# A two-layer fp32 trunk with split weights: the low part of one weight tile in four made by an accumulating DMA

## The chip, the cores and the metric

One core of a Trainium2 chip runs the whole program as one launch. The metric is the device time of one execution in microseconds (us).

## The reference

`x` is a residual stream of 256 tokens by 2048 channels; there are two layers. In each, the RMS-normalised input is projected by one matrix of 20480 columns into the parts of two token mixers and two gates. Differential attention (8 heads of two softmaxes each) and stick-breaking attention (16 heads) run beside each other; each result is gated by SiLU and projected to 2048 channels; the two are merged by sigmoid gates and projected once more onto the residual:

```python
h = rms_norm(x, norm_gain)
(da_q, da_k, da_v, da_z, sb_q, sb_k, sb_v, sb_z, gate_a, gate_b) = split_columns(h @ w_in)   # 10 x 2048
oa = differential_attention(rope(rms_norm(q)), rope(rms_norm(k)), va, lam)
ua = (rms_norm(oa) * (1 - lambda_init)) * silu(da_z)
ub = stick_breaking_attention(qs, ks, vs) * silu(sb_z)
y = sigmoid(gate_a) * (ua @ w_branch_a) + sigmoid(gate_b) * (ub @ w_branch_b)
x = x + y @ w_out
```

All inputs, weights and outputs are float32.

## The kernel before

The program is written for a tile framework: it names tiles in pools with so many slots each, and a scheduler sets the order of instructions on each engine and the semaphores between them. A slot of a pool is used again when all readers of its old tile are done.

**Numbers in three products.** Each float32 operand of a matmul is held as a high part (the value cast to float32r) and a low part (value minus high part, again float32r). `mm3` (lines 64 to 67) sums three products in PSUM: high x high (L65), high x low (L66) and low x high (L67).

**Weights.** All weight matrices lie in HBM as tiles of 128 partitions by 1024 float32 (512 KB): two 128-row blocks of 512 output columns. `load_w` (lines 76 to 88) takes one such tile through three steps: SyncE loads it into `wraw` (L83), ScalarE casts it to the high part `wh` (L61), VectorE subtracts to get the low part `wl` (L62). `wraw` has four slots, `wh` and `wl` three each; the split stands at a higher priority than its place in the program.

**Projections.** `project` (lines 90 to 107) computes 256 tokens by 512 columns. It walks through 8 weight tiles (kp = 0 to 7), each used for 12 matmuls of 128x128 by 128x512: two 128-row blocks, two token tiles, three products. In the text "tile 0" to "tile 7" of a projection are these. There are 104 projections, 52 per layer, one after the other: for each of four column groups the q, k, v and z parts of differential attention; then for each group q, k, z and v of stick-breaking attention; then, for each of four column groups, gate a with `w_a`, then gate b with `w_b`; then four of `w_o`. The attention work of a group (scores, softmax, transposes) is put by the scheduler among the matmuls of the projections that follow. The stages are called differential attention, stick-breaking attention, merge and output below.

**GpSimd** has little to do: the small chains `rv`, `rr` of the norms (L127, L130), two of the products of the rotary embedding (`tok`, L260 and L262), and eight stores of the next layer's input (`x_next`, L480). `work` holds six slots of token tiles `tok` (128x512).

Of the kernel before, what the change touches and what calls it, by code (L numbers as in the profile page):

```python
# [9 lines left out]
F32 = mybir.dt.float32  # L10
F32R = mybir.dt.float32r
AF = mybir.ActivationFunctionType
ALU = mybir.AluOpType
# [3 lines left out]
P = 128  # L17
# [5 lines left out]
CW = 512  # L23
NG = D // CW
KK = 2
# [13 lines left out]
def trunk(ctx: ExitStack, tc: tile.TileContext, x, xT, gT, norm_gain, w_in, qk_gain, lam_vecs,  # L39
          subln, w_a, w_b, w_o, rope_cs, out):  # L40
    nc = tc.nc

    const = ctx.enter_context(tc.tile_pool(name="const", bufs=1))
    big = ctx.enter_context(tc.tile_pool(name="big", bufs=1))
    wp = ctx.enter_context(tc.tile_pool(name="wp", bufs=3))
    att = ctx.enter_context(tc.tile_pool(name="att", bufs=1))
    work = ctx.enter_context(tc.tile_pool(name="work", bufs=6))
    small = ctx.enter_context(tc.tile_pool(name="small", bufs=4))
    dram = ctx.enter_context(tc.tile_pool(name="dram", bufs=1, space=bass.MemoryType.DRAM))
    ps_mm = ctx.enter_context(tc.tile_pool(name="ps_mm", bufs=4, space=PSUM))  # L50
# [3 lines left out]
    def heads(ap):  # L54
        return ap.rearrange("p (h d) -> p h d", d=HD)
# [4 lines left out]
    def split(h, l, src):  # L60
        nc.scalar.copy(h, src)  # L61
        nc.vector.tensor_tensor(out=l, in0=src, in1=h.bitcast(F32), op=ALU.subtract)  # L62

    def mm3(ps, lh, ll, rh, rl, start, stop):
        nc.tensor.matmul(ps, lhsT=lh, rhs=rh, start=start, stop=False)  # L65
        nc.tensor.matmul(ps, lhsT=lh, rhs=rl, start=False, stop=False)  # L66
        nc.tensor.matmul(ps, lhsT=ll, rhs=rh, start=False, stop=stop)  # L67
# [5 lines left out]
    gcol = const.tile([P, KT], F32, name="gcol")  # L73
    nc.scalar.dma_start(out=gcol, in_=gT)

    def load_w(src, parts=1, between=None):
        raw = wp.tile([P, KK * CW], F32, name="wraw", bufs=4)
        h = wp.tile([P, KK * CW], F32R, name="wh")
        l = wp.tile([P, KK * CW], F32R, name="wl")
        n = KK * CW // parts  # L80
        for i in range(parts):
            c = slice(i * n, (i + 1) * n)
            nc.sync.dma_start(out=raw[:, c], in_=src[:, c])  # L83
            if between is not None and i == 0:
                between()
            with tc.high_priority(offset=400):
                split(h[:, c], l[:, c], raw[:, c])
        return h, l
# [20 lines left out]
    def pair(tag):  # L109
        return (big.tile([P, KT, S], F32R, name=tag + "h", tag=tag + "h"),  # L110
                big.tile([P, KT, S], F32R, name=tag + "l", tag=tag + "l"))

    def put_T(src, dst, c, t):
        """Four 128x128 blocks of src, transposed and split, into k-tiles 4c.. of dst."""
        tr = ps_tr.tile([P, CW], F32, name="tr")
        for j in range(CW // P):
            nc.tensor.transpose(out=tr[:, j * P:(j + 1) * P], in_=src[:, j * P:(j + 1) * P],  # L117
                                identity=ident)
        js, ts = slice(c * 4, c * 4 + 4), slice(t * P, (t + 1) * P)
        trv = heads(tr)  # L120
        split(dst[0][:, js, ts], dst[1][:, js, ts], trv)

    def rsqrt_mean(ss, n):
        """(ss / n + eps) ** -0.5"""
        w = ss.shape[1]
        v = small.tile([P, 4], F32, name="rv")
        nc.gpsimd.tensor_scalar(out=v[:, :w], in0=ss, scalar1=1.0 / n, scalar2=RMS_EPS,  # L127
                                op0=ALU.mult, op1=ALU.add)
        r = small.tile([P, 4], F32, name="rr")
        nc.gpsimd.tensor_tensor(out=r[:, :w], in0=v[:, :w], in1=mhalf[:, :w], op=ALU.pow)  # L130
        return r[:, :w]

# [1 line left out]
    xt = pair("xT")  # L134
    ss_part = small.tile([P, NT, NG], F32, name="ss_part", bufs=2)
    sq_junk = const.tile([P, CW], F32, name="sq_junk")
# [45 lines left out]
    for l in range(DEPTH):  # L182
        lam_init = 0.8 - 0.6 * math.exp(-0.3 * l)

# [1 line left out]
        rope = {}  # L186
        g4 = work.tile([P, CW], F32, name="tok")
        nc.sync.dma_start(out=g4, in_=qk_gain[l:l + 1, :].broadcast_to([P, CW]))
# [23 lines left out]
        nc.vector.tensor_tensor(out=nlam, in0=le[:, 1:2], in1=le[:, 0:1], op=ALU.subtract)  # L212
        nc.vector.tensor_scalar(out=nlam, in0=nlam, scalar1=-lam_init, scalar2=None, op0=ALU.add)

# [1 line left out]
        ssx = small.tile([P, NT], F32, name="ssx", bufs=2)  # L216
        nc.vector.tensor_reduce(out=ssx, in_=ss_part, axis=AX.X, op=ALU.add)
        rstd = small.tile([P, NT], F32, name="rstd", bufs=2)
        nc.vector.tensor_copy(rstd, rsqrt_mean(ssx, D))
        rstd_s = small.tile([P, NT], F32, name="rstd_s", bufs=2)  # L220
        nc.vector.tensor_scalar(out=rstd_s, in0=rstd, scalar1=QK_SCALE, scalar2=None, op0=ALU.mult)
# [73 lines left out]
            return gz  # L295

        def scores(qT, kT, hs, t, mask):
            """Masked scores of heads hs for query tile t: [128, len(hs) * keys]."""
            nk = (t + 1) * P
            sc = ps_sc.tile([P, CW], F32, name="sc")  # L300
            for i, h in enumerate(hs):
                ts = slice(t * P, (t + 1) * P)
                mm3(sc[:, i * nk:(i + 1) * nk], qT[0][:, h, ts], qT[1][:, h, ts],
                    kT[0][:, h, :nk], kT[1][:, h, :nk], True, True)
            w = len(hs) * nk
            sm = work.tile([P, CW], F32, name="tok")
            mk = mask[:, S - nk:].unsqueeze(1).broadcast_to([P, len(hs), nk])
            nc.vector.tensor_tensor(out=sm[:, :w].rearrange("p (h k) -> p h k", k=nk),
                                    in0=sc[:, :w].rearrange("p (h k) -> p h k", k=nk),
                                    in1=mk, op=ALU.add)  # L310
            return sm, nk

        def attn_pair():
            """Transposed weights, split: per head the blocks (query tile, key tile) 00, 10, 11."""
            return (att.tile([P, HPG, 3, P], F32R, name="aTh"),
                    att.tile([P, HPG, 3, P], F32R, name="aTl"))

        def attn_T(a, aT, hs, t):
            """a: [128, heads hs, key tiles 0..t] of query tile t."""
            tr = ps_tr.tile([P, CW], F32, name="tr")  # L320
            w = len(hs) * (t + 1) * P
            for j in range(0, w, P):
                nc.tensor.transpose(out=tr[:, j:j + P], in_=a[:, j:j + P], identity=ident)  # L323
            hh, bb = slice(hs[0], hs[-1] + 1), slice(t, 2 * t + 1)
            split(aT[0][:, hh, bb], aT[1][:, hh, bb],
                  tr[:, :w].rearrange("p (h b k) -> p h b k", b=t + 1, k=P))

# [1 line left out]
        for g in range(NG):  # L329
            qT = da_qk("q", g)  # L330
            kT = da_qk("k", g)
            aT = attn_pair()
            for t in range(NT):
                nk = (t + 1) * P
                for hs in ([[0, 1, 2, 3]] if t == 0 else [[0, 1], [2, 3]]):
                    sm, _ = scores(qT, kT, hs, t, masks["causal"])
                    n = len(hs)
# [5 lines left out]
                    sums = small.tile([P, HPG], F32, name="sums")  # L343
# [8 lines left out]
                    a = work.tile([P, CW], F32, name="tok")  # L352
# [31 lines left out]
                nc.vector.tensor_tensor(out=u, in0=hold[:, t], in1=gz[:, t], op=ALU.mult)  # L384
                put_T(u, ua, g, t)

# [1 line left out]
        for g in range(NG):  # L388
            qT = sb_qk("q", g)
            kT = sb_qk("k", g)  # L390
# [2 lines left out]
            for t in range(NT):  # L393
                for hs in ([[0, 1, 2, 3]] if t == 0 else [[0, 1], [2, 3]]):
                    sm, nk = scores(qT, kT, hs, t, masks["strict"])
                    e = work.tile([P, CW], F32, name="tok")
                    nc.scalar.activation(out=e, in_=sm, func=AF.Abs)
                    nc.scalar.activation(out=e, in_=e, func=AF.Exp, scale=-1.0)
                    nc.scalar.activation(out=e, in_=e, func=AF.Ln, bias=1.0)
                    rl = work.tile([P, CW], F32, name="tok")  # L400
                    nc.vector.tensor_scalar(out=rl, in0=sm, scalar1=0.0, scalar2=None, op0=ALU.max)
                    for i in range(len(hs)):
                        lo, hi = i * nk, (i + 1) * nk
                        rv = slice(hi - 1, lo - 1 if lo else None, -1)
                        nc.vector.tensor_tensor_scan(out=e[:, rv], data0=e[:, rv], data1=rl[:, rv],
                                                     initial=0.0, op0=ALU.add, op1=ALU.add)
                    nc.vector.tensor_tensor(out=sm, in0=sm, in1=e, op=ALU.subtract)
                    nc.scalar.activation(out=sm, in_=sm, func=AF.Exp)
                    attn_T(sm, wT, hs, t)
            gz = act_proj(SB_Z, g, AF.Silu)  # L410
            gzT = att.tile([P, HPG, S], F32, name="gzT", tag="hold")
            for t in range(NT):
                tr = ps_tr.tile([P, CW], F32, name="tr")
                for h in range(HPG):
                    nc.tensor.transpose(out=tr[:, h * P:(h + 1) * P],  # L415
                                        in_=gz[:, t, h * P:(h + 1) * P], identity=ident)
                nc.scalar.copy(gzT[:, :, t * P:(t + 1) * P], heads(tr))
            vh, vl = v_proj(SB_V, g)
            for hp in range(0, HPG, 2):
                o = ps_sc.tile([P, CW], F32, name="sc")  # L420
                ov = o.rearrange("p (h q) -> p h q", q=S)
                for i in range(2):
                    h = hp + i
# [9 lines left out]
                ks = slice(g * 4 + hp, g * 4 + hp + 2)  # L433
                split(ub[0][:, ks], ub[1][:, ks], uv)

# [1 line left out]
        ya = [att.tile([P, NT, CW], F32, name="ya", tag=tag) for tag in ("qTh", "qTl", "kTh", "kTl")]  # L437
        for c in range(NG):
            gz = act_proj(GATE_A, c, AF.Sigmoid)
# [11 lines left out]
                nc.vector.tensor_tensor(out=y, in0=y, in1=ya[c][:, t], op=ALU.add)  # L451
                put_T(y, yT, c, t)

# [1 line left out]
        last = l == DEPTH - 1  # L455
        if not last:
            x_next = dram.tile([S, D], F32, name="x_next")
# [2 lines left out]
        for c in range(NG):  # L460
# [7 lines left out]
            for t in range(NT):  # L468
                xn = work.tile([P, CW], F32, name="tok")
                n = 2 if last and c == NG - 1 and t == NT - 1 else 1  # L470
                for i in range(n):
# [3 lines left out]
                    if last:  # L475
                        eng = nc.scalar if i else nc.sync
                        eng.dma_start(out=out[t * P:(t + 1) * P, c * CW + w.start:c * CW + w.stop],
                                      in_=xn[:, w])
# [60 lines left out]
```

## Time and profile before

| | |
|---|---|
| time, median of 2 runs | 2438.73 us (2438.55 to 2438.91) |
| span of the profiled execution | 2436.2 us |
| TensorE busy | 2427.0 us (100%), 11328 matmuls |
| VectorE busy | 1430.3 us (59%) |
| ScalarE busy | 1257.7 us (52%) |
| GpSimd busy | 179.7 us (7%) |
| moved by DMA | 453.39 MB, mean 186 GB/s |

The profiled execution's own time is its span, 2436.2 us from the first to the last instruction; it lies 2.5 us under the median of the runs. In the rows of the profile PE is TensorE (PEld its weight loads), DVE is VectorE, ACT is ScalarE, POOL is GpSimd, SP is SyncE, and a q behind a name is the queue that issues DMAs. A row of a group gives line, engine, operation, output<-input, count, then busy time and mean ns of one, then the idle time before it and what ended that. A row of the timeline gives start, duration, engine, line, and in brackets the idle time before it with its releaser.

### The profile page before, as it was taken

The page shows a single profiled execution, that of the slowest core. Times are in us where ns is not written, and L with a number is a line of the kernel's source. Part 1 is how long each engine was busy: PE and PEld are TensorE (multiplying, and loading weights), DVE is VectorE, ACT ScalarE, POOL GpSimd, SP SyncE. Part 2 cuts the span into 40 slices and gives each one's busy share as a digit, 9 for nine tenths or more (in the row PEclk, how much of TensorE's full clock was granted, in tenths as well). Part 3 has the DMA queues.
Part 4 walks back from the last instruction along what each step waited for, and adds up shares of the span by engine and source line. Part 5 has one row for each costly group of instructions (what it writes and reads, how often), then busy time and mean ns, then how long its engine had stood idle before and what let it go on. Part 6 is the DMA issues. An engine that isn't in the chain of part 4 may idle for free.

```text
span 2436.2 us, 29977 instructions
## 1 busy us (share of the span) xinstructions
PE 2427.0 (100%) x11328; PEld 2019.4 (83%) x11328; DVE 1430.3 (59%) x1636; ACT 1257.7 (52%) x1771; POOL 179.7 (7%) x183
## 2 busy tenths in 40 slices
PE   9999999999999999999999999999999999999999
PEld 7888888888888888888888888888888888888887
DVE  7676766655656444555566757656556564445554
ACT  6555655645645444444455555556556454444443
POOL 2031130000000000000030321300000000000000
PEclk9999999999999999999999999999999999999999
DMA  8555555555555555556755555555555555555565
GB/s 291 170 174 179 173 179 179 175 176 171 172 179 174 196 191 195 191 192 201 240 199 173 176 179 173 173 182 173 173 174 173 182 173 192 196 191 191 189 206 182
DMA packets 128386, 453.39 MB, mean 186 GB/s; under 512 B 14321, under 2 KB 15089, under 8 KB 128241
## 3 DMA queue, kind: packets, MB, share of 16 engines
q1 hardware_dynamic: 127312, 449.24, 55.5%
q8 instruction: 89, 1.46, 0.3%
q0 software_dynamic: 640, 2.10, 0.2%
q14 instruction: 57, 0.46, 0.1%
q10 hardware_dynamic: 288, 0.14, 0.0%
HBM read 447.23 MB, written 4.19 MB: 185 GB/s over the span
## 4 chain that ended last, share of the span: by engine, by line
PE 99%; DMA 0%; SPq 0%; DVE 0%; ACT 0%; issue 0%; DVEq 0%
PE mm L66 31%; PE mm L67 31%; PE mm L65 31%; PE tr L117 2%; PE sc L67 1%; PE sc L66 1%; PE sc L65 1%; PE tr L323 1%; PE tr L415 0%; DMA wraw<-in_w_in 0%; DVE wl L62 0%; ACT wh L61 0%; SPq L148 0%; SPq L83 0%; SPq L141 0%; DVE tok L473 0%
## 5 line engine op out<-in xcount | busy, mean ns | idle before, releaser
L62 DVE TENSOR_TENSOR wl<-wraw,wh 128x1024 fp32r<-128x1024 f32 (+1 forms) x833 | 1026.3, 1232 | 838.1 <-ACT wh L61 837.5
L61 ACT CAST wh<-wraw 128x1024 fp32r<-128x1024 f32 (+1 forms) x833 | 875.7, 1051 | 969.8 <-PE mm L67 946.0
L66 PE MATMUL mm<-wl,xTh 128*128 128x512 f32 x2560 | 1004.6, 392 | 0.5 <-DVE wl L62 0.5
L67 PE MATMUL mm<-wh,xTl 128*128 128x512 f32 x2560 | 1004.6, 392 | 0.0
L65 PE MATMUL mm<-wh,xTh 128*128 128x512 f32 x2560 | 930.4, 392 | 4.6 <-DVE xTh L149 4.4
L65 PEld LDWEIGHTS mm<-wh,xTh 128*128 128x128 f32 x2560 | 480.5, 188 | 101.7 <-ACT wh L61 5.3
L66 PEld LDWEIGHTS mm<-wl,xTh 128*128 128x128 f32 x2560 | 481.5, 188 | 96.7 <-DVE wl L62 1.1
L67 PEld LDWEIGHTS mm<-wh,xTl 128*128 128x128 f32 x2560 | 481.5, 188 | 95.4
L66 PE MATMUL mm<-wl,uah 128*128 128x512 f32 x512 | 199.6, 390 | 0.0
L67 PE MATMUL mm<-wh,ual 128*128 128x512 f32 x512 | 199.3, 389 | 0.0
L65 PE MATMUL mm<-wh,uah 128*128 128x512 f32 x512 | 180.1, 390 | 0.0
L65 PEld LDWEIGHTS mm<-wh,uah 128*128 128x128 f32 x512 | 96.1, 188 | 19.9
L67 PEld LDWEIGHTS mm<-wh,ual 128*128 128x128 f32 x512 | 96.1, 188 | 19.8
L66 PEld LDWEIGHTS mm<-wl,uah 128*128 128x128 f32 x512 | 96.1, 188 | 19.7
L66 PE MATMUL mm<-wl,ubh 128*128 128x512 f32 x256 | 99.6, 389 | 0.0
L67 PE MATMUL mm<-wh,ubl 128*128 128x512 f32 x256 | 99.6, 389 | 0.0
L65 PE MATMUL mm<-wh,ubh 128*128 128x512 f32 x256 | 89.2, 389 | 0.0
L480 POOL DMA_DIRECT2D x_next<-tok x8 | 4.5, 567 | 828.8 <-DVE tok L473 828.8
L127 POOL TENSOR_SCALAR rv<-ssq 128x4 f32<-128x4 f32 (+1 forms) x48 | 26.7, 556 | 523.7 <-ACT sq_junk L372 272.5
L117 PEld LDWEIGHTS tr<-ident,tok 128*128 128x128 f32 x416 | 51.2, 140 | 12.5
L117 PE MATMUL tr<-ident,tok 128*128 128x128 f32 x416 | 60.9, 272 | 0.0
L130 POOL TENSOR_TENSOR rr<-rv,mhalf 128x4 f32<-128x4 f32 (+1 forms) x50 | 57.9, 1157 | 4.2
(115 smaller groups left out, 1524.8 us busy)
## 6 DMA issues: line engine op xcount, KB each, us to landing
wraw<-in_w_in SPq DMA_DIRECT2D x639, 512.0 KB, 3.3
wraw<-in_w_a SPq DMA_DIRECT2D x64, 512.0 KB, 3.3
wraw<-in_w_b SPq DMA_DIRECT2D x64, 512.0 KB, 3.3
wraw<-in_w_o SPq DMA_DIRECT2D x64, 512.0 KB, 3.9
tok<-in_x SPq DMA_DIRECT2D x8, 256.0 KB, 6.8
xr<-in_x SPq DMA_DIRECT2D x4, 512.0 KB, 5.6
x_next<-tok POOLq DMA_DIRECT2D x8, 256.0 KB, 5.2
xr<-x_next SPq DMA_DIRECT2D x4, 512.0 KB, 5.4
```

Source lines behind the costliest of these rows:

```text
L61: nc.scalar.copy(h, src)
L62: nc.vector.tensor_tensor(out=l, in0=src, in1=h.bitcast(F32), op=ALU.subtract)
L65: nc.tensor.matmul(ps, lhsT=lh, rhs=rh, start=start, stop=False)
L66: nc.tensor.matmul(ps, lhsT=lh, rhs=rl, start=False, stop=False)
L67: nc.tensor.matmul(ps, lhsT=ll, rhs=rh, start=False, stop=stop)
L117: nc.tensor.transpose(out=tr[:, j * P:(j + 1) * P], in_=src[:, j * P:(j + 1) * P], identity=ident)
L127: nc.gpsimd.tensor_scalar(out=v[:, :w], in0=ss, scalar1=1.0 / n, scalar2=RMS_EPS, op0=ALU.mult, op1=ALU.add)
L130: nc.gpsimd.tensor_tensor(out=r[:, :w], in0=v[:, :w], in1=mhalf[:, :w], op=ALU.pow)
L323: nc.tensor.transpose(out=tr[:, j:j + P], in_=a[:, j:j + P], identity=ident)
L480: nc.gpsimd.dma_start(out=x_next[t * P:(t + 1) * P, cs], in_=xn)
```

## The change

One weight tile in four gets its low part in another way. ScalarE casts the raw tile to `wh` as before, then writes minus `wh` into `wl`; then GpSimd issues a DMA that adds the raw values onto `wl`, so that `wl` holds raw minus high. For every second of these tiles the DMA reads the values from HBM again, for the others from the `wraw` slot in SBUF. The count starts so that these are tiles 0 (from HBM) and 4 (from SBUF) of each projection; the very first tile of the program, which is loaded in two pieces, is split as before. That makes 103 tiles of the first kind and 104 of the second. `wh` and `wl` have four slots, `wraw` three, and `work` five.

```diff
-    wp = ctx.enter_context(tc.tile_pool(name="wp", bufs=3))
+    wp = ctx.enter_context(tc.tile_pool(name="wp", bufs=4))
...
-    work = ctx.enter_context(tc.tile_pool(name="work", bufs=6))
+    work = ctx.enter_context(tc.tile_pool(name="work", bufs=5))
...
+    loads = [0]
+
     def load_w(src, parts=1, between=None):
-        raw = wp.tile([P, KK * CW], F32, name="wraw", bufs=4)
+        raw = wp.tile([P, KK * CW], F32, name="wraw", bufs=3)
         h = wp.tile([P, KK * CW], F32R, name="wh")
         l = wp.tile([P, KK * CW], F32R, name="wl")
         n = KK * CW // parts
+        loads[0] += 1
+        if parts == 1 and loads[0] % 4 == 1:
+            nc.sync.dma_start(out=raw, in_=src)
+            with tc.high_priority(offset=400):
+                nc.scalar.copy(h, raw)
+                nc.scalar.mul(l, h.bitcast(F32), -1.0)
+                if loads[0] % 8 == 1:
+                    nc.gpsimd.dma_start(out=l, in_=src, accum_op=ALU.add)
+                else:
+                    nc.gpsimd.dma_start(out=l, in_=raw, accum_op=ALU.add)
+            return h, l
         for i in range(parts):
```

What else the diff holds takes out comments. Line numbers of the changed kernel are 10 to 13 higher than those of before.

**ScalarE, in the merge stage** (`wh_` and `wl_` are numbered weight tiles, `gz` the gate's activation; a bracket names whose semaphores an instruction waits for, DMAHW those of loads, DMASW those of GpSimd's DMAs). Before, casts of weight tiles follow each other:

```order
L61 CAST wh_7121<-wraw_7120 128x1024 [waits DMAHW0_49,DVE_49,PE_49]
L61 CAST wh_7144<-wraw_7143 128x1024 [waits DMAHW1_49,DVE_49,PE_49]
L61 CAST wh_7162<-wraw_7161 128x1024 [waits DMAHW2_49,DVE_49,PE_49]
L294 ACTIVATE gz_7138<-mm_6992,rstd_357 128x512 [waits PE_49]
L61 CAST wh_7180<-wraw_7179 128x1024 [waits DMAHW3_49,DVE_49,PE_49]
```

Now, at the same place, the first cast of the projection (L87) has the negated copy (L88) behind it:

```order
L61 CAST wh_7190<-wraw_7189 128x1024 [waits DMAHW0_49,DVE_49,PE_49]
L87 CAST wh_7213<-wraw_7212 128x1024 [waits DMAHW1_49,PE_49,Activation_49]
L88 ACTIVATE wl_7214<-wh_7213 128x1024 [waits DMASW4_49,Activation_49]
L61 CAST wh_7232<-wraw_7231 128x1024 [waits DMAHW2_49,DVE_49,PE_49]
L61 CAST wh_7250<-wraw_7249 128x1024 [waits DMAHW3_49,DVE_49,PE_49]
L307 ACTIVATE gz_7207<-mm_7059,rstd_358 128x512 [waits PE_49]
```

The negated copy stands right behind its cast, and what followed the cast comes one instruction later.

**SyncE, the loads at the same place.** Before, each load of a raw tile waits for VectorE, the last reader of the slot's old tile:

```order
L83 DMA wraw_7102<-in_w_in 128x1024 [waits DMAHW3_49,DVE_49]
L83 DMA wraw_7120<-in_w_in 128x1024 [waits DMAHW4_49,DVE_49]
L83 DMA wraw_7143<-in_w_a 128x1024 [waits DMAHW5_49,DVE_49]
L83 DMA wraw_7161<-in_w_a 128x1024 [waits DMAHW6_49,DVE_49]
L83 DMA wraw_7179<-in_w_a 128x1024 [waits DMAHW7_49,DVE_49]
```

Now (L85 loads tiles 0 and 4, L96 the others; the row with `wraw_7134` is a tile 4, the row with `wraw_7212` the next tile 0):

```order
L85 DMA wraw_7134<-in_w_in 128x1024 [waits DMAHW2_49,DVE_49]
L96 DMA wraw_7153<-in_w_in 128x1024 [waits DMAHW3_49,DVE_49]
L96 DMA wraw_7171<-in_w_in 128x1024 [waits DMAHW4_49,DVE_49]
L96 DMA wraw_7189<-in_w_in 128x1024 [waits DMAHW6_49,DVE_49]
L85 DMA wraw_7212<-in_w_a 128x1024 [waits DMAHW5_49,DMASW4_49]
L96 DMA wraw_7231<-in_w_a 128x1024 [waits DMAHW7_49,DVE_49]
```

The load of the next tile 0 waits for a DMA of GpSimd, the one that read the raw tile 4, and the loads behind it wait with it. It is so for tile 0 in 70 of 103 projections; in the other 33 the load of tile 7 has that wait, and tile 0 stands behind it.

**GpSimd, in differential attention after a k projection.** Before (`rv` and `rr` are the norm of one token tile each, `tok` the rotary products):

```order
L127 TENSOR_SCALAR rv_1424<-ssq_1419 128x4 [waits Activation_49]
L130 TENSOR_TENSOR rr_1426<-rv_1424,mhalf_318 128x4 [waits Pool_49]
L260 TENSOR_TENSOR tok_1434<-tok_1430,t1_k_340 128x4x64 [waits DMAHW3_49,DVE_49]
L262 TENSOR_TENSOR tok_1434<-tok_1430,t1_k_340 128x4x64
L127 TENSOR_SCALAR rv_1450<-ssq_1445 128x4 [waits Activation_49]
L130 TENSOR_TENSOR rr_1452<-rv_1450,mhalf_318 128x4 [waits Pool_49]
L260 TENSOR_TENSOR tok_1460<-tok_1456,t1_k_340 128x4x64 [waits DVE_49,PE_49]
L262 TENSOR_TENSOR tok_1460<-tok_1456,t1_k_340 128x4x64
```

Now (L90 is the DMA of the next projection's tile 0, L92 that of its tile 4):

```order
L90 DMA wl_1576<-in_w_in 128x1024 [waits DMASW2_49,PE_49,Activation_49]
L140 TENSOR_SCALAR rv_1435<-ssq_1430 128x4 [waits Activation_49]
L143 TENSOR_TENSOR rr_1437<-rv_1435,mhalf_319 128x4 [waits Pool_49]
L140 TENSOR_SCALAR rv_1461<-ssq_1456 128x4 [waits Activation_49]
L143 TENSOR_TENSOR rr_1463<-rv_1461,mhalf_319 128x4 [waits Pool_49]
L273 TENSOR_TENSOR tok_1445<-tok_1441,t1_k_341 128x4x64 [waits DVE_49]
L275 TENSOR_TENSOR tok_1445<-tok_1441,t1_k_341 128x4x64
L92 DMA wl_1649<-wraw_1647 128x1024 [waits DMASW3_49,DMAHW3_49,PE_49,Activation_49]
L273 TENSOR_TENSOR tok_1471<-tok_1467,t1_k_341 128x4x64 [waits DVE_49,Pool_49]
L275 TENSOR_TENSOR tok_1471<-tok_1467,t1_k_341 128x4x64
```

The second token tile's `rv` and `rr` have moved ahead of the first one's products, and the DMA of tile 4 stands between the products of the first and of the second token tile.

## The prediction

> **What bounds the kernel now.** I read the page's busy table, the clock line and the chain of waits first.
>
> ```profile
> PE 2427.0 (100%) x11328; PEld 2019.4 (83%) x11328; DVE 1430.3 (59%) x1636; ACT 1257.7 (52%) x1771; POOL 179.7 (7%) x183
> ...
> PEclk9999999999999999999999999999999999999999
> ...
> PE 99%; DMA 0%; SPq 0%; DVE 0%; ACT 0%; issue 0%; DVEq 0%
> ```
>
> TensorE is busy 2427.0 of 2436.2 us at full granted clock, and 99% of the chain is TensorE. The change leaves every matmul in place. So the most it can win is the 9 us in which TensorE is not busy (0.4%), and what it can lose is open: a weight tile that comes late stops TensorE for as long as it is late. Everything below is therefore about lateness. The two groups that prepare a weight tile come next, with what they wait for, and then the rhythm in the merge stage, where nothing else mixes in.
>
> ```profile
> L62 DVE TENSOR_TENSOR wl<-wraw,wh 128x1024 fp32r<-128x1024 f32 (+1 forms) x833 | 1026.3, 1232 | 838.1 <-ACT wh L61 837.5
> L61 ACT CAST wh<-wraw 128x1024 fp32r<-128x1024 f32 (+1 forms) x833 | 875.7, 1051 | 969.8 <-PE mm L67 946.0
> ```
>
> ```profile
> 1102.93 0.61 PE L65 MATMUL mm<-wh,xTh 128*128 128x512 f32 x2
> 1103.13 1.05 ACT L61 CAST wh<-wraw 128x1024 fp32r<-128x1024 f32 x1 [1.67 <-PE mm L67]
> ...
> 1103.38 0.39 PE L66 MATMUL mm<-wl,xTh 128*128 128x512 f32 x1
> ...
> 1104.21 1.23 DVE L62 TENSOR_TENSOR wl<-wraw,wh 128x1024 fp32r<-128x1024 f32 x1 [1.50 <-ACT wh L61]
> ...
> 1105.65 0.61 PE L65 MATMUL mm<-wh,xTh 128*128 128x512 f32 x2
> ```
>
> Both preparing engines wait: ScalarE for TensorE to leave a slot (946 us), VectorE for ScalarE (837.5 us). Neither is near its limit. A tile lasts 1105.65 - 1102.93 = 2.72 us on TensorE. The cast of a new tile starts 0.20 us after TensorE has moved to the next one (a slot came free), and the low part is first needed 0.45 us into its tile (the L66 at 1103.38). With three slots the cast at 1103.13 serves the tile that starts two tiles after 1102.93, at 1108.37; its low part is done at 1105.44, so each tile is ready about 3.4 us before it is needed.
>
> **The change, part by part.** There are 832 tiles (833 splits, the first tile in two pieces), 8 to a projection, 104 projections. Tile 0 of each projection but the first takes its low part by an accumulating DMA from HBM (103 times), tile 4 of each by one from the raw tile in SBUF (104 times).
>
> *Removed from VectorE:* 207 subtractions of 1.23 us, 255 us. VectorE waits already; worth nothing.
>
> *Added to ScalarE:* 207 negated copies. The nearest row is the cast of the same shape, 1.05 us, so 217 us, which the 946 us of waiting for TensorE hides; if that cover were gone, all 217 us would show. What counts is that 1.05 us stands in each accumulated tile's chain.
>
> *Four slots instead of three:* the cast may start when TensorE has three tiles to go: budget 3 x 2.72 + 0.45 = 8.61 us from a tile's start to the need. From it go 0.20 (slot), 1.05 (cast), 1.05 (negated copy) and about 0.1 for two hand-overs (the row pair 1103.13 + 1.05 to 1104.21 shows 0.03 for one). **So the accumulating DMA has 6.2 us from its issue to land**, where the subtraction needed 1.23. That is the first number that decides.
>
> *How long it takes.* Before has no accumulating DMA. Its nearest rows, from the table of DMA issues, the issue line of L480, and the last 16 us (no load in flight any more):
>
> ```profile
> q1 hardware_dynamic: 127312, 449.24, 55.5%
> ...
> wraw<-in_w_in SPq DMA_DIRECT2D x639, 512.0 KB, 3.3
> ...
> x_next<-tok POOLq DMA_DIRECT2D x8, 256.0 KB, 5.2
> ...
> out<-tok SPq DMA_DIRECT2D x7, 256.0 KB, 5.9
> ```
>
> ```profile
> DMA to landing us min/median/max: 4.7/5.2/7.0
> ```
>
> ```profile
> out<-tok SPq DMA_DIRECT2D x1, 256.0 KB, 2.6
> ```
>
> Queue q1 moved 449.24 MB in 55.5% of 2436.2 us of the 16 engines, 332 GB/s, so 512 KB is 1.58 us and 256 KB 0.79 us of transfer. GpSimd's own plain store of 256 KB took 5.2 us beside weight loads. An accumulating 512 KB must read its source and its old destination; I count that as two transfers, 3.16 us, or 2.4 more than the store: 5.2 + 2.4 = **7.6 us** beside loads. The same store from SyncE fell from 5.9 to 2.6 us where no load ran, so alone I count 2.6 + 2.4 = 5.0 us. The ends I keep: 3.3 us (a plain load of that size, no extra cost) and 7.0 + 2.4 = 9.4 us (the slowest store). The form that reads the raw tile runs about half of its time beside loads, since with three raw slots SyncE then has no free slot: the middle of 5.0 and 7.6, **6.3 us**. The form that reads HBM runs beside the loads that were held back: 7.6 us.
>
> The Trainium skill puts a GpSimd-issued DMA at about 2.0 us plus bytes / 436 GB/s ("DMA: Bandwidth & Descriptors", "Anatomy of one DMA — SWDGE (gpsimd) path"), and says of the adding unit that it costs a second source read and no cycles of its own ("Collectives: The Full Stack", "The bandwidth ceiling: the fold count and why AG ≠ RS ≠ AR"). By both the accumulate would be an estimated 2.0 + 2.4 = 4.4 us and nearly all of the loss below would vanish. The x_next row disagrees with the first: 5.2 us where that formula gives 2.6.
>
> *Tile 4 (raw form):* 6.3 against 6.2: 0.1 us late, 104 x 0.1 = 10 us.
>
> *Three raw slots, and tile 4 holds its slot until its DMA has landed.* By the order on SyncE, 70 times the next tile 0 takes that slot, and 33 times tile 7 does, with tile 0 queued behind it. Tile 4 lands when TensorE needs it; call that 0. In the 70: load 3.4, cast 1.05, negated copy and hand-overs 1.2: the HBM-form DMA is issued at 5.7, and TensorE wants the result four tiles later, at 10.9: budget 5.2. At 7.6 it is 2.4 us late: 70 x 2.4 = 168 us. In the 33 the load is second in line behind tile 7's (1.58 more) and budget is 3.7: 33 x 3.9 = 129 us.
>
> *GpSimd's queue in differential attention.* After a q or k projection of that branch (16 of them) the order puts tile 4's DMA of the next projection behind two rv/rr pairs and two tok products. The rows of layer 1's first q, whose projection ended at 1242.7:
>
> ```profile
> 1242.71 0.37 ACT L241 ACTIVATE sq_junk<-mm,rstd 128x128 f32<-128x128 f32 x1 [0.53 <-PE mm L67]
> ...
> 1247.75 0.37 ACT L241 ACTIVATE sq_junk<-mm,rstd 128x128 f32<-128x128 f32 x1
> 1248.02 0.20 ACT L241 ACTIVATION_READ_ACCUMULATOR sq_junk<-mm,rstd 128x1 f32 x1
> ```
>
> ```profile
> 1245.53 0.87 POOL L127 TENSOR_SCALAR rv<-ssq 128x4 f32<-128x4 f32 x1 [19.99 <-ACT sq_junk L241]
> 1246.48 1.01 POOL L130 TENSOR_TENSOR rr<-rv,mhalf 128x4 f32<-128x4 f32 x1
> 1248.68 1.59 POOL L260 TENSOR_TENSOR tok<-tok,t_q 128x256 f32<-128x256 f32 x1 [1.19 <-issue]
> 1250.24 1.19 POOL L262 TENSOR_TENSOR tok<-tok,t_q 128x256 f32<-128x256 f32 x1
> 1251.51 0.69 POOL L127 TENSOR_SCALAR rv<-ssq 128x4 f32<-128x4 f32 x1
> 1252.29 1.86 POOL L130 TENSOR_TENSOR rr<-rv,mhalf 128x4 f32<-128x4 f32 x1
> ```
>
> The second rv can start when the second squares end, 1248.2; with 0.69, 1.86, 1.59 and 1.19 behind it the DMA is issued at about 1253.6, 10.9 us after the projection's end; the need is 4 x 2.72 + 0.45 = 11.3 after it. 10.9 + 6.3 - 11.3 = 5.9 us late, 5.8 more than counted: 16 x 5.8 = 93 us. Behind the waiting DMA stand the other two tok products, whose k or q TensorE needs later.
>
> *Against it: attention work.* Between tiles TensorE also has 2427.0 - 832 x 2.72 = 164 us of scores, transposes and values in the 64 attention projections, 2.56 us each. It lengthens budgets; about half falls into tile 0's chain (4 tiles of 8): -82 us.
>
> *Five work tiles for six:* each reuse of a token tile may wait sooner; on VectorE and ScalarE with over 800 us of slack I count nothing; a late transpose would cost up to the 82 us above.
>
> Sum: 10 + 168 + 129 + 93 - 82 = 318 us. The profiled span is 2436.2; the median of the two runs, 2438.7, lies 2.5 above it. 2438.7 + 318 = **2757 us**, 13% slower.
>
> **Rivals.** *In time (not slower).* The DMA without the contention that I put in lands in 5.0 us or less, in both forms. For it: the 2.6 us store when alone, and the 3.3 us load; against it: the 5.2 us of the only GpSimd DMAs here. Tile 4 is then 1.2 us early, which frees the raw slot earlier; budgets become 6.4 and 4.9, and tile 0 is in time. What is left is GpSimd's queue, 16 x (10.9 + 5.0 - 11.3) = 74 us, less the attention cover: 2439 to 2487, about 2455. The point from which it decides is about 5 us for the landing. It is the rule of the skill, above, that points this way (4.4 us).
>
> *The accumulate is much slower than two transfers.* If its price goes by bytes from the 5.2 us store (2 x 5.2 + 1.58 = 12 us), lateness is 5.8 at tile 4, 6.8 or 8.3 at tile 0: 104 x 5.8 + 70 x 6.8 + 33 x 8.3 + 11 = 1364 us, about 3800 us. For it: nothing here shows the adding path's rate. Against it: in the 5.2 us only 0.8 is transfer.
>
> *Faster.* Only the 9 us without TensorE could go: 2430 at best.
>
> **How the numbers follow.** Forecast (late by some us at most projections): 0.62. Its own range: with both landings 1.3 us sooner (5.0 and 6.3) only the 33 and the queue are left (33 x 1.4 + 74 - 82 = 38), about 2477; with 9.4 us for both, 104 x 3.2 + 70 x 4.2 + 33 x 5.7 + 93 - 82 = 826, so 3265. In time: 0.26. Much slower: 0.11. Faster: 0.01. The range takes the forecast and the in-time case, 2436 to 3265. A measurement of this kernel tells about 2% from no change (2390 to 2487): faster 0.01, same 0.26, slower 0.73.
>
> **What would show it.** VectorE's L62 must lose 207 instructions and ScalarE gain as many negated copies of near 1.05 us. In the issue table the landing time of the two wl DMAs decides: near 6 (from the raw tile) and 7.6 (from HBM) if I am right, 5 or less for the in-time case, 10 or more for the slow one. TensorE's L66 should wait on those DMAs, tile 0 more than tile 4, and in differential attention tile 4 most. ScalarE's cast of tile 0 should wait for its raw tile. I would be wrong on the mechanism if TensorE waits for the DMAs little while the time rises, or if the loads themselves slow down and plain tiles come late.

## The result, and the profile after

| | before | changed |
|---|---|---|
| time, median of 2 runs | 2438.73 us | 2582.25 us (2582.24 to 2582.26) |
| ratio | | 1.0589 (95% 1.0558 to 1.0620) |
| span of the profiled execution | 2436.2 us | 2580.4 us |

The change costs 143 us, 5.9%. The forecast had the direction and the range, but 318 us: more than twice the loss. The busy row, the row of GpSimd's queue and the chain of the changed kernel's page:

```profile
PE 2476.2 (96%) x11328; PEld 2031.2 (79%) x11328; DVE 1192.7 (46%) x1429; ACT 1475.9 (57%) x1986; POOL 296.7 (11%) x390
...
q0 software_dynamic: 30448, 110.64, 24.0%
...
PE 28%; DMA 13%; ACT 3%; issue 1%; DVE 0%; POOL 0%; ACTq 0%; DVEq 0%; POOLq 0%
```

The chain was 99% TensorE; now it passes through DMAs. The span grew by 144.2 us in two parts. TensorE is not busy for 2580.4 - 2476.2 = 104.2 us where it was 9.2: 95.0 us. And the same 11328 matmuls keep it busy 49.2 us longer. What TensorE waits for, from the changed kernel's waits (total us, times, longest):

```profile
PE mm L66 <- DMA wl<-in_w_in: 58.4, 50, 3.9
PE mm L66 <- DMA wl<-in_w_o: 10.9, 7, 2.5
PE mm L66 <- DMA wl<-in_w_a: 8.8, 7, 2.2
PE mm L66 <- DMA wl<-wraw: 8.3, 4, 7.5
PE mm L66 <- DMA wl<-in_w_b: 7.3, 7, 2.2
```

The first, second, third and fifth row are the tile 0 that reads HBM: 85.4 us in 71 of 103 cases. The tile 4 that reads the raw tile (fourth row) makes TensorE wait 4 times in 104. The table of DMA issues says why the two differ (last number: median us from issue to landing):

```profile
wraw<-in_w_in SPq DMA_DIRECT2D x639, 512.0 KB, 4.3
wl<-wraw POOLq DMA_DIRECT2D x104, 512.0 KB, 4.7
wl<-in_w_in POOLq DMA_DIRECT2D x79, 512.0 KB, 6.5
...
wl<-in_w_a POOLq DMA_DIRECT2D x8, 512.0 KB, 7.1
wl<-in_w_b POOLq DMA_DIRECT2D x8, 512.0 KB, 7.0
wl<-in_w_o POOLq DMA_DIRECT2D x8, 512.0 KB, 7.3
```

The loads of raw tiles slowed too, from 3.3 to 4.3 us, but TensorE doesn't wait for plain tiles: such waits come to 1.4 us in the whole run.

One tile 0 in the merge stage, from the timeline of the changed kernel (its last row is the first matmul after it):

```profile
1072.59 1.05 ACT L87 CAST wh<-wraw 128x1024 fp32r<-128x1024 f32 x1 [1.71 <-PE mm L67]
...
1073.68 1.06 ACT L88 ACTIVATE wl<-wh 128x1024 fp32r<-128x1024 f32 x1
...
1075.03 0.87 POOL L90 DMA_DIRECT2D wl<-in_w_b  x1 [10.95 <-ACT wl L88]
...
1081.71 0.50 PE L66 MATMUL mm<-wl,ubh 128*128 128x512 f32 x1 [0.59 <-DMA wl<-in_w_b]
```

Cast and negated copy take 1.05 and 1.06 us as forecast. The DMA is issued at 1075.03, 2.44 us after the cast began. TensorE wanted the low part 0.59 us before it got it at 1081.71, at about 1081.1. So the DMA had some 6 us from issue to need. A landing of 4.7 us fits into that; one of 6.5 to 7.3 us doesn't.

The 49.2 us of longer busy time have two causes that the trace shows. The first is the clock. These are stretches of the changed kernel (us, then for TensorE, its weight loads, VectorE, ScalarE and GpSimd the busy time and count, then the granted clock, DMA share, GB/s):

```profile
741.10:744.51 3.41, 1.54 (x7) 0.99 (x6) 1.23 (x1) 1.63 (x2) 0.00 (x0) 1.00 0.89 291
744.51:747.93 3.42, 3.42 (x9) 2.66 (x9) 0.00 (x0) 0.04 (x1) 0.00 (x0) 0.50 0.56 192
747.90:752.00 4.10, 4.10 (x23) 3.37 (x23) 0.69 (x2) 3.19 (x5) 0.86 (x1) 1.00 0.08 16
...
1724.14:1727.56 3.42, 1.68 (x8) 1.06 (x6) 1.93 (x2) 2.23 (x3) 0.00 (x0) 1.00 1.02 285
1727.56:1730.97 3.41, 2.64 (x12) 2.19 (x13) 0.14 (x1) 0.00 (x0) 0.00 (x0) 1.00 0.75 286
```

The first stretch holds a stall of 1.87 us, and behind it the clock was granted at half for 3.4 us: 9 matmuls there, 23 in the 4.1 us after it. A longer stall, 2.52 us from 1725.81 to 1728.33, was followed by no half clock. The difference is where they lie. All 14 stretches of half clock in this trace begin a whole number of 3.413 us after the first of them, so these lengths of 3.413 us form a fixed grid. Each of the 14 follows a length of this grid in which TensorE was idle for 1.76 us or more. After the program's first, the most idle time that was followed by full clock is 1.74 us: it belongs to the stall of 2.52 us, which the grid cuts into 1.74 and 0.77 us. In split3 (below) the border is less sharp: 1.77 us was followed by half clock and 1.94 us was not. The mean granted clock of the execution fell from 1.000 to 0.989:

```profile
core 0: 2580.4 us, clock 0.989
```

The 14 stretches last 54.6 us together and lose half of it, 27 us.

The second cause is at the edges of each stall, here the one of 1.87 us:

```profile
741.29 0.61 PE L65 MATMUL mm<-wh,xTh 128*128 128x512 f32 x2
743.77 0.50 PE L66 MATMUL mm<-wl,xTh 128*128 128x512 f32 x1 [1.87 <-DMA wl<-in_w_in]
744.11 0.40 PE L67 MATMUL mm<-wh,xTl 128*128 128x512 f32 x1
```

In the steady stream a matmul starts 0.23 us after the one before it, though its row lasts 0.39 us: the rows overlap, and the pair at 741.29 takes 0.61. Before a stall the last row runs to its end with no other over it, 0.16 us more. After the stall the second matmul starts 0.34 us behind the first, 0.11 us more. With some 0.27 us for each of the 76 waits in the table of TensorE's waits this is an estimated 21 us, and 27 + 21 is nearly all of the 49.2 us.

### The profile page after: what moved, and what is told of

Read it like the earlier page. It is cut to its first block, busy times and chain, and to the rows that moved or that the text cites. A ratio compares the mean times of both kernels' runs of the same rounds, so it can differ in the third digit from the quotient of the medians.

```text
span 2580.4 us, 30488 instructions
## 1 busy us (share of the span) xinstructions
PE 2476.2 (96%) x11328; PEld 2031.2 (79%) x11328; DVE 1192.7 (46%) x1429; ACT 1475.9 (57%) x1986; POOL 296.7 (11%) x390
## 3 DMA queue, kind: packets, MB, share of 16 engines
q0 software_dynamic: 30448, 110.64, 24.0%
## 5 line engine op out<-in xcount | busy, mean ns | idle before, releaser
L62 DVE TENSOR_TENSOR wl<-wraw,wh 128x1024 fp32r<-128x1024 f32 (+1 forms) x626 | 768.4, 1229 | 1126.0 <-ACT wh L61 1125.7
L66 PE MATMUL mm<-wl,xTh 128*128 128x512 f32 x2560 | 1019.4, 398 | 67.1 <-DMA wl<-in_w_in 58.4
L61 ACT CAST wh<-wraw 128x1024 fp32r<-128x1024 f32 (+1 forms) x626 | 656.7, 1049 | 637.2 <-PE mm L67 410.9
L65 PE MATMUL mm<-wh,xTh 128*128 128x512 f32 x2560 | 986.6, 394 | 5.4 <-DVE xTh L162 4.5
L65 PEld LDWEIGHTS mm<-wh,xTh 128*128 128x128 f32 x2560 | 485.2, 190 | 104.2 <-ACT wh L61 6.4
L87 ACT CAST wh<-wraw 128x1024 fp32r<-128x1024 f32 x207 | 217.5, 1051 | 299.4 <-PE mm L67 256.4
L88 ACT ACTIVATE wl<-wh 128x1024 fp32r<-128x1024 f32 x207 | 219.5, 1060 | 6.3
L92 POOL DMA_DIRECT2D wl<-wraw x104 | 91.1, 876 | 977.8 <-ACT wl L88 857.9
L65 PE MATMUL mm<-wh,uah 128*128 128x512 f32 x512 | 196.4, 394 | 0.0
L90 POOL DMA_DIRECT2D wl<-in_w_in x79 | 69.4, 879 | 816.8 <-ACT wl L88 672.8
L66 PEld LDWEIGHTS mm<-wl,ubh 128*128 128x128 f32 x256 | 48.0, 188 | 21.1 <-DMA wl<-in_w_b 10.3
```

The costliest lines, as they stand in the source:

```text
L87: nc.scalar.copy(h, raw)
L88: nc.scalar.mul(l, h.bitcast(F32), -1.0)
L90: nc.gpsimd.dma_start(out=l, in_=src, accum_op=ALU.add)
L92: nc.gpsimd.dma_start(out=l, in_=raw, accum_op=ALU.add)
```

## The experiments

Each is an edit of the changed kernel and was timed beside the kernel before on the same chip (2439 to 2440 us there).

| kernel | edit | us | ratio to before (95%) | granted clock |
|---|---|---|---|---|
| pools_only | only the pool sizes | 2440.56 | 1.0003 (0.9993 to 1.0013) | 0.999 |
| vector_add | VectorE adds, no DMA | 2441.79 | 1.0009 (0.9999 to 1.0019) | 1.000 |
| tile0_only | HBM form alone | 2524.69 | 1.0350 (1.0335 to 1.0366) | 0.997 |
| tile4_only | raw form alone | 2456.62 | 1.0071 (1.0056 to 1.0086) | 0.997 |
| plain_dma | DMAs copy, don't add | 2454.36 | 1.0060 (1.0045 to 1.0075) | 0.998 |
| hbm_tile2 | HBM form on tile 2 | 2565.35 | 1.0517 (1.0501 to 1.0533) | 0.995 |
| all_raw | both tiles by the raw form | 2506.49 | 1.0279 (1.0262 to 1.0297) | 0.996 |
| all_hbm | both tiles by the HBM form | 2563.10 | 1.0497 (1.0463 to 1.0531) | 0.996 |
| raw4 | a fourth raw slot | 2568.31 | 1.0527 (1.0510 to 1.0545) | 0.993 |
| all_raw4 | all_raw with a fourth raw slot | 2502.56 | 1.0261 (1.0245 to 1.0276) | 0.991 |
| pools_raw4 | pools of raw4, no DMA | 2440.13 | 0.9999 (0.9989 to 1.0008) | 0.999 |
| split3 | three split slots | 3001.67 | 1.2297 (1.2251 to 1.2344) | 0.945 |
| halves | the DMAs in two halves | 2513.74 | 1.0308 (1.0292 to 1.0323) | 0.997 |
| raw_halves | all_raw in two halves | 2582.22 | 1.0593 (1.0567 to 1.0619) | 0.993 |

**The pools without the DMAs, and the adding on VectorE.** pools_only takes the plain path for every tile; vector_add keeps the four and three slots, the negated copy and its place, and lets VectorE add.

```diff
-        if parts == 1 and loads[0] % 4 == 1:
+        if False:
```

```diff
-                if loads[0] % 8 == 1:
-                    nc.gpsimd.dma_start(out=l, in_=src, accum_op=ALU.add)
-                else:
-                    nc.gpsimd.dma_start(out=l, in_=raw, accum_op=ALU.add)
+                nc.vector.tensor_tensor(out=l, in0=raw, in1=l.bitcast(F32), op=ALU.add)
```

> The slots of the change (four wh and wl, three wraw, five tok) and no accumulated tile: every low part comes from VectorE as before. If lateness of the accumulated tiles is the whole loss: 2439 us, within 5, TensorE full. If the pools cost something by themselves (three raw slots feed the casts too late): 2450 us or more, with TensorE waiting for casts or subtractions.

> ScalarE writes minus the high part for one tile in four as in the change, but VectorE adds the raw tile onto it in place of the DMA; same slots. Both theories: 2439 us, within 5, since only the DMA's time makes the tile late. If the negated copy on ScalarE is what delays the casts of the other tiles: 2460 us or more, with TensorE waiting for plain tiles.

Neither differs from before by more than 0.2%. The page of vector_add:

```profile
PE 2427.0 (99%) x11328; PEld 2018.7 (83%) x11328; DVE 1432.1 (59%) x1636; ACT 1489.1 (61%) x1994; POOL 137.4 (6%) x183
```

ScalarE has its 207 negated copies and TensorE is busy exactly as long as before. So the new pool sizes, three raw slots, five work tiles and the longer chain on ScalarE cost nothing by themselves. The loss is in the DMAs.

**One form at a time.** Tile 0 alone (`% 8 == 1`), tile 4 alone (`% 8 == 5`); the other tile takes the plain path.

```diff
-        if parts == 1 and loads[0] % 4 == 1:
+        if parts == 1 and loads[0] % 8 == 1:
```

> Only tile 0 of each projection is accumulated, from HBM (103 tiles); tile 4 is split by VectorE, so no raw slot is held by a DMA. Theory A, the DMA from HBM takes longer (6.5 to 7.3 us) than the about 6 us that four slots give: most of the loss stays, 2530 to 2580 us, and TensorE waits for wl from HBM about 70 times. Theory B, tile 4's DMA holds the raw slot and tile 0's load comes late for it: the loss goes, 2440 to 2455 us.

> Only tile 4 of each projection is accumulated, from the raw tile in SBUF (104 tiles); tile 0 is split by VectorE. Theory A: it lands in 4.7 us, inside its 6 us, so 2440 to 2455 us, with a rest from GpSimd's queue in differential attention (the changed kernel shows 14 waits, 21 us). Theory B: the same, since a split tile 0 has over 3 us of slack. If the loss comes with every accumulated tile alike (ScalarE's extra copy, contention of the DMA engines): half of it, about 2510 us.

The HBM form alone costs 85 us, the raw form alone 17. (The 14 waits and 21 us that the second expectation quotes add TensorE's weight loads, 10 and 12.5 us, to its matmuls, 4 and 8.3 us; the four are among the ten.) Who waited for the DMA of tile 0 in tile0_only, and its landing:

```profile
  PE mm L66: 62.3, 61
...
DMA to landing us min/median/max: 5.0/6.6/8.5
```

The waits of tile4_only, of TensorE and of ScalarE:

```profile
PE mm L66 <- DMA wl<-wraw: 12.5, 8, 5.0
...
ACT wh L61 <- DMA wraw<-in_w_in: 235.8, 116, 5.1
```

The slot that tile 4 holds is real: ScalarE's casts now wait 235.8 us for raw tiles. But plain tiles follow in tile4_only, whose subtraction needs 1.23 us instead of a DMA, so TensorE does not see it. Together the forms cost 143, 41 us more than 85 + 17.

**The same DMAs without the adding.** Both `accum_op` are taken away; the low part is then a copy of the raw tile, so this kernel leaves the subtraction out.

```diff
-                    nc.gpsimd.dma_start(out=l, in_=src, accum_op=ALU.add)
+                    nc.gpsimd.dma_start(out=l, in_=src)
```

> The change with GpSimd's 207 DMAs as plain copies: no adding, the output's low parts are raw values there. It prices the adding path. If the add costs one more transfer, as I counted (1.6 us): landing about 3.1 us from the raw tile and 5.0 from HBM, all in time, 2440 to 2455 us. If the add costs next to nothing and the time is GpSimd's issue and the sharing of the DMA engines: landings stay at 4.7 and 6.5 to 7, and the time at 2570 to 2590 us.

Issues and queue of plain_dma:

```profile
q0 software_dynamic: 30448, 110.64, 13.1%
...
wl<-wraw POOLq DMA_DIRECT2D x104, 512.0 KB, 2.9
wl<-in_w_in POOLq DMA_DIRECT2D x79, 512.0 KB, 4.7
```

It lands 1.8 us sooner in both forms (2.9 against 4.7, 4.7 against 6.5), and 128 of the 143 us are gone. The queue tells the same: the same 110.64 MB took 13.1% of 2452.8 us here and 24.0% of 2580.4 us with the adding, 321 and 619 us of the 16 engines. With 110.64 MB / 0.524 = 211 transfers of 512 KB, that is 1.5 us a transfer against 2.9. With the add a transfer takes the engines about as long as two, as counted in the prediction (1.58 and 3.16). The Trainium skill's rule of a second source read ("Collectives: The Full Stack", "The bandwidth ceiling: the fold count and why AG ≠ RS ≠ AR") agrees with these rows. Its 2.0 us plus bytes / 436 GB/s ("DMA: Bandwidth & Descriptors", "Anatomy of one DMA — SWDGE (gpsimd) path") is an estimated 3.2 us for a plain 512 KB: near the 2.9 us inside SBUF, and too low for the 4.7 us from HBM.

**One split slot fewer.** `wp` has three slots, as before.

```diff
-    wp = ctx.enter_context(tc.tile_pool(name="wp", bufs=4))
+    wp = ctx.enter_context(tc.tile_pool(name="wp", bufs=3))
```

> The change with three slots of wh and wl instead of four: one tile, 2.72 us, less lead for every accumulated tile, the DMAs as they are. If lead against landing is the mechanism: about 3.3 us are left after ScalarE's two steps; the raw form (4.7) is 1.4 us late 104 times and the HBM form (6.7) 3.4 us 103 times, 146 + 350 = 496 us: 2900 to 3000 us, more with half-clock stretches. If the landing adapts (less is in flight while TensorE waits): 2700 to 2850 us.

3001.67 us: a slot less is a tile less of lead, 2.72 us. Waits of split3:

```profile
PE mm L66 <- DMA wl<-in_w_in: 205.8, 74, 5.0
PE mm L66 <- DMA wl<-wraw: 92.3, 81, 6.9
```

With some 6 - 2.7 = 3.3 us from issue to need the raw form is late too, in 81 cases, and the HBM form in nearly all: 74 of 79 in these matrices. The lead sets the loss. The clock of this kernel is 0.945: 0.055 x 3008.5 = 165 us of its span are clock alone.

**HBM form away from the held slot.** A tile 0 waits for a load that the DMA of tile 4 holds up; the load of tile 2 does not wait for that DMA.

```diff
-        if parts == 1 and loads[0] % 4 == 1:
+        if parts == 1 and loads[0] % 8 in (3, 5):
...
-                if loads[0] % 8 == 1:
+                if loads[0] % 8 == 3:
```

> The change with the HBM form on tile 2 in place of tile 0; tile 4 stays in the raw form. The load of tile 2 comes before tile 4 and is not held back by it; the plain tile 0 behind the held slot has over 3 us of slack. tile0_only lost 85 us and tile4_only 17, both together 143: 41 us are from the two beside each other. If the held raw slot makes them: about 2439 + 85 + 17 = 2541 us. If it is only more DMA traffic or more clock loss from more stalls: unchanged, 2570 to 2590 us.

2565.35 us, 17 less than the change, and nearer to the value for no relief. Who waited for its HBM form, and the landing:

```profile
  PE mm L66: 85.0, 73
...
DMA to landing us min/median/max: 5.1/7.0/8.8
```

TensorE waits as long as in the changed kernel. But the two DMAs now stand two tiles apart instead of four, and the landings are longer (7.0 against 6.8 us, in the raw form 5.3 against 4.7), so this run does not isolate the slot.

**One form for both tiles.** The inner test becomes `if False:` (all_raw) or `if True:` (all_hbm).

> Tiles 0 and 4 both accumulated from the raw tile in SBUF. Theory A (landing against lead): it lands in about 4.7 us, and also where the slot before it is held it has 5.2 us or more: 2450 to 2480 us, with twice the few late tiles of tile4_only. Theory B (held slots decide): slots are held twice as often, each accumulated tile's load waits for the one before: 2580 us or more.

> Tiles 0 and 4 both accumulated from HBM, no slot held by a DMA. Theory A: every one of 207 is late by what tile0_only shows (0.7 us in the mean of 103, more with more traffic), plus clock loss: 2439 + 2 x 85 = 2609 us or more, up to 2680. Theory B: no slot is held, so no worse than tile0_only, 2525 us.

Both lie between their rivals' numbers. all_raw loses 67 us, where two tiles in time would have lost about 2 x 17. Waits of all_raw:

```profile
PE mm L66 <- DMA wl<-wraw: 38.9, 37, 5.6
...
ACT wh L61 <- DMA wraw<-in_w_in: 332.8, 138, 6.7
ACT wh L87 <- DMA wraw<-in_w_in: 70.5, 74, 3.2
```

Here the casts of the accumulated tiles themselves (L87) wait for raw tiles, which the plain path would have hidden. all_hbm, with landings of 6.4 to 7.4 us, loses 124 us, less than the 143 of the mixed form, though all its DMAs are of the slow kind; no DMA holds a raw slot there, which fits the loss but was not taken apart further.

**A fourth raw slot.** Paid for by smaller `work` and `small` pools and a bfloat16 junk tile; all_raw4 is all_raw with the same pools, pools_raw4 these pools with no accumulated tile.

```diff
-        raw = wp.tile([P, KK * CW], F32, name="wraw", bufs=3)
+        raw = wp.tile([P, KK * CW], F32, name="wraw", bufs=4)
...
-    work = ctx.enter_context(tc.tile_pool(name="work", bufs=5))
-    small = ctx.enter_context(tc.tile_pool(name="small", bufs=4))
+    work = ctx.enter_context(tc.tile_pool(name="work", bufs=4))
+    small = ctx.enter_context(tc.tile_pool(name="small", bufs=3))
```

> The change with four raw slots (made room for by four tok slots, three of the small ones, and the junk output of the squares in bf16; what is computed stays). A held raw slot no longer delays tile 0's load. If held slots make the part of the loss that the two forms have only together: 2439 + 85 + 17 = 2541 us. If the HBM form's landing against its lead is all: unchanged, 2570 to 2590. Under 2500 us would say that the held slot was the main cause.

> all_raw (both tiles from SBUF, 2506 us) with four raw slots in the same way. There the landing of 4.8 us is within the lead, so what was lost should be the held slots: 2445 to 2465 us. If it stays at 2500, the loss there is contention or a longer chain, not the slot.

> The pools of raw4 (four raw slots, four tok slots, three of the small ones, bf16 junk) and no accumulated tile. If the 25 us of waiting of transposes in raw4 come from the smaller pools: 2460 to 2470 us, and raw4 without that cost is about 2541 us, so the held slot is worth about 40 us of the change's loss. If the pools alone cost nothing: 2439 us, and the held slot is worth only the 14 us seen.

Waits of TensorE in raw4:

```profile
PE mm L66 <- DMA wl<-in_w_in: 42.6, 41, 2.6
PE tr L336 <- ACT tok L421: 24.0, 8, 3.1
...
PE mm L66 <- DMA wl<-in_w_o: 5.4, 6, 1.3
PE mm L66 <- DMA wl<-in_w_a: 5.1, 6, 1.4
...
PE mm L66 <- DMA wl<-in_w_b: 3.6, 6, 1.5
```

The wait for tile 0 falls from 85.4 us (71 times) to 56.7 (59); in all_raw4 that for both falls from 38.9 (37) to 16.1 (11). So the held slot is worth 23 to 29 us of TensorE's waiting; tile0_only, where no slot is held, has 62.3 us (61) and agrees. In time little comes back (14 and 4 us), because transposes now wait 24 us for a token tile (L336), and in all_raw4 the clock fell as well, from 0.996 to 0.991. That wait is absent in pools_raw4, which runs as fast as before: it comes from the smaller pools together with the accumulated tiles. The price of the slot in time stays open to that extent.

**Two halves.** Cast, negated copy and DMA for half a tile at a time, so that the first half is issued sooner; raw_halves does so with the raw form for both tiles. In halves the first half is issued 1.97 us after the first cast began, in the median, where a whole tile took 2.44 us; the second is issued after 2.50 us, since ScalarE does both casts before the negated copies.

```diff
+                for c in (slice(0, CW), slice(CW, KK * CW)):
+                    nc.scalar.copy(h[:, c], raw[:, c])
+                    nc.scalar.mul(l[:, c], h[:, c].bitcast(F32), -1.0)
+                    nc.gpsimd.dma_start(out=l[:, c], in_=(src if loads[0] % 8 == 1 else raw)[:, c],
+                                        accum_op=ALU.add)
```

> The change with each accumulated tile cast, negated and added in two halves of 256 KB, one per 128-row block. The first half's DMA can be issued about 0.6 us earlier and has half to move (about 1.7 us less by the plain and adding landings), and the second is needed 1.36 us later than the first. Lead against landing: most lateness goes, 2445 to 2490 us. If each GpSimd DMA has a fixed price that two of them pay twice, or the traffic is what costs: 2560 us or more.

> Tiles 0 and 4 both in the raw form (2506 us as whole tiles) and in two halves each, three raw slots. The first half's DMA is issued 0.6 us earlier and moves half. If lead against landing: 2450 to 2480 us. If the held slot or the number of GpSimd DMAs is what costs: 2500 us or more.

halves gains 68 us on the change and misses its number all the same. GpSimd's issue of a half and its landing in halves:

```profile
L90 POOL DMA_DIRECT2D wl<-in_w_in x158: 859/922/1236, 34.0 to 2369.0; - x158
...
wl<-in_w_in POOLq DMA_DIRECT2D x158, 256.0 KB, 6.3
```

Issuing a half takes as long as issuing a whole (0.92 against 0.87 us). In the HBM form the first halves land after a median of 6.0 us and the second after 6.9 (whole tiles 6.8), in the raw form after 3.3 and 4.6 (whole tiles 4.7): the first half gains in issue and landing, the second only by being needed 1.36 us later. raw_halves is a miss in the other direction, 76 us slower than all_raw. Its waits, SyncE's queue and ScalarE's and TensorE's:

```profile
SPq L95 <- DMA wl<-wraw: 426.0, 65, 8.5
...
ACT wh L61 <- DMA wraw<-in_w_in: 456.6, 156, 7.7
...
PE tr L129 <- DVE tok L276: 28.7, 13, 3.6
```

The raw slot is held until the second of two DMAs has landed, and loads wait for that up to 8.5 us, 426.0 us in all (in all_raw up to 8.0 us, 319.8 us in all). TensorE waits 28.7 us for transposes (5.2 in all_raw) and 55.5 us for low parts (38.9). Why the transposes come late was not taken apart. No version beats before: TensorE was full, and no edit takes work from it.

## Why the prediction was right or wrong, step by step

- **What bounds the kernel** was right. VectorE's 207 subtractions are gone (1636 to 1429 instructions, 1430.3 to 1192.7 us) and nothing was won.
- **Added to ScalarE** was right: 1.06 us each, 215 more instructions in all, hidden; vector_add shows the same work at no cost.
- **Four slots: 6.2 us from issue to need** was nearly right: some 6 us in the rows above. The hand-over to GpSimd took 1075.03 - 1074.74 = 0.29 us where 0.1 stood for two. split3 shows that this lead is what counts.
- **How long it takes** is the first of two steps that failed. The doubling was right: 1.4 us more of the engines, 1.8 us more to the landing, against 1.58. The base was wrong. I took 5.2 us from GpSimd's store of `x_next`, whose destination is HBM, and added for size. Plain copies into SBUF took 2.9 us from SBUF and 4.7 from HBM, with twice the bytes of that store. So the landings were 4.7 instead of 6.3 us (raw form) and 6.5 to 7.3 instead of 7.6 (HBM form). Whether the destination or the other traffic at those eight stores made them slow, no run tells.
- **Tile 4, 10 us**, is near the row (8.3 us) by luck. 7.5 us of the row are one wait for the program's first tile 4, and the other three come to 0.8 us. The tile is not 0.1 us late each time, but by the medians 6 - 4.7 = 1.3 us early, and 100 of 104 cost TensorE no wait.
- **The held raw slot, 168 + 129 us**, was mis-sized. Without a held slot the same sum gives 103 x (7.6 - 6.2) = 144 us, so it puts 153 us on the slot, where raw4 shows 29 us of waiting. One reason is the landing: with tile 4 early the slot comes free 6.2 - 4.7 = 1.5 us sooner. The other is that the held slot shortened the lead by little. The 207 casts of L87 waited 132 times for TensorE to leave a split slot (256.4 us) and 44 times for a raw tile (42.8 us, about 1 us each). From the issue to the first weight load that wants the low part, tile 0 had a median of 5.7 us in the 70 cases and in the others alike, where the sum has budgets of 5.2 and 3.7 us. The DMA of L90 in the changed kernel lands after a median of 6.8 us:

```profile
DMA to landing us min/median/max: 5.3/6.8/8.2
```

  So tile 0 is about 1.1 us late in the median, and TensorE's waits for it come to 85.4 us.
- **GpSimd's queue, 93 us**, is the second: it did not come. After a q projection of differential attention, in the timeline of the changed kernel:

```profile
1328.13 0.72 POOL L275 TENSOR_TENSOR tok<-tok,t_q 128x256 f32<-128x256 f32 x1
...
1332.52 0.93 POOL L92 DMA_DIRECT2D wl<-wraw  x1 [3.66 <-ACT wl L88]
```

  GpSimd had finished its products and waited 3.66 us for the negated copy, which here came late itself, behind a stall of 2.76 us at tile 0 and half clock. But in all 104 cases the DMA of tile 4 was issued at most 1.22 us after the negated copy had ended (median 0.29), and at most 1.23 us in tile4_only, where no tile 0 stalls TensorE. GpSimd's products were shorter than the sum has them: the one at 1328.13 took 0.72 us, the prediction's row of the same product 1.19 (see the last section).
- **The cover by attention work, -82 us**, can't be told apart; 32 of 103 tile 0 cost TensorE no wait, and the rest were less late than the sum has them.
- **What was missing:** the price of a stall beyond the wait itself. 27 us of the 143 are lost in half-clock stretches and an estimated 21 us at the edges of the stalls, together a third of the loss.
- **The rivals.** In time was true of the raw form alone (landing under 5 us, 17 us lost). The point from which it decides, about 5 us, agrees with the runs: 4.7 us fits, 6.5 does not. Much slower (price by bytes, 12 us) falls with the landings of 4.7 to 7.3 us. The 41 us by which both forms together cost more than each alone are partly the held slot (23 to 29 us of waiting) and partly the lower clock (0.989 against 0.997 in each alone); how much of each stays open.

## What to carry to other kernels

Before handing a step of a full pipeline to a DMA, compare the lead (slots times tile time, less the preparing chain) with the landing, and price the landing from a row with the same source and destination: here a 256 KB store to HBM (5.2 us) misled about 512 KB copies into SBUF (2.9 and 4.7 us). An accumulating DMA took the DMA engines twice as long as a plain one (2.9 against 1.5 us), so a plain copy that only just fits does not leave room for it. Taking work off an engine that waits already brings nothing, and on a TensorE that never stopped each short stall can cost clock on top of the wait.

## What the runs showed of the hardware that I had not expected

- **A short stall can halve the clock, and where it lies decides.** A stall of 1.87 us was followed by 3.4 us at 0.50 and one of 2.52 us was not (rows above); what counted in the changed kernel was idle time of more than about 1.75 us within one length of a fixed grid of 3.413 us, and split3's mean clock is 0.945. The 3.4 us agree with the window of the Trainium skill ("TensorE: Matmul & The Clock Gate", "What's actually happening"); its rule that gaps have to stay under some 3.4 us ("HAM oscillation — how this bites in real kernels") is too mild here, since 1.87 us sufficed.
- **Adding lengthens the issue too.** GpSimd's issue took 0.55 us in plain_dma and 0.87 with the adding; half the bytes did not shorten it (0.92 for a half tile):

```profile
L92 POOL DMA_DIRECT2D wl<-wraw x104 | 57.6, 554 | 907.9 <-ACT wl L88 800.2 <-ACT aTh L61 95.3 <-PE mm L67 12.4
```

- **GpSimd's products became shorter, for a reason that stays open.** These are the same 16 products in before, in the changed kernel and in vector_add (behind the bar: busy us, mean ns):

```profile
L260 POOL TENSOR_TENSOR tok<-tok,t_q 128x256 f32<-128x256 f32 x16 | 22.0, 1375 | 17.7 <-DVE tok L250 16.5 <-issue 1.2
```

```profile
L273 POOL TENSOR_TENSOR tok<-tok,t_q 128x256 f32<-128x256 f32 x16 | 13.9, 870 | 0.0
```

```profile
L270 POOL TENSOR_TENSOR tok<-tok,t_q 128x256 f32<-128x256 f32 x16 | 18.3, 1143 | 5.1 <-DVE tok L260 4.4 <-POOL tok L272 0.6
```

  1375 ns became 870 while VectorE went from 59% to 46% busy. But in vector_add VectorE is 59% busy as before, and they take 1143 ns. So VectorE's share of busy time alone doesn't explain it; the order on GpSimd changed too, and neither was tried by itself.
